# Partial sums of the Strassen products read out of one PSUM chain, the second row factor moved into the final norm, and no GpSimd sums in the feed-forward part

## The chip, the cores and the metric

The kernel runs on one core of a Trainium2 chip. The metric is the device time of one execution in microseconds. The engines are TensorE (PE; its weight loads are PEld), VectorE (DVE), ScalarE (ACT), GpSimd (POOL) and SyncE (SP), which issues the DMAs.

## What is computed

One decoder layer runs on 1024 prompt tokens and 8 sample tokens with common weights, T = 1032 columns in all: a mixer (pooling and convolution), cross attention, a gated feed-forward, and a final RMSNorm. The change lies in the last two:

```python
def rmsnorm(x, g):
    xf = x.astype(jnp.float32)
    y = xf * lax.rsqrt(jnp.mean(xf * xf, axis=-1, keepdims=True) + EPS)
    return (y * g.astype(jnp.float32)).astype(x.dtype)
...
    x = x + cross_attn(rmsnorm(x, g_attn), mk, mv, w_q, w_o)
    h = rmsnorm(x, g_ffn)
    x = x + (jax.nn.silu(h @ w_gate) * (h @ w_up)) @ w_down
...
y_prompt = rmsnorm(xp, g_final)
y_sample = rmsnorm(xs, g_final)
```

D_MODEL is 1024 and D_FF is 2816, that is FF_TILES = 22 tiles of 128.

## The kernel before, in words

**Layout.** Channels lie on the 128 partitions and tokens along the free axis. Every matrix operand is split into a high and a low half (`split`, L343 to L362: the high half by ScalarE at L351 or GpSimd at L353, the low half, a subtraction, at L362), and a product is three matmuls, one for each pair in `PASSES`. The tokens are cut in two column halves of 512 and 520.

**Feed-forward, first matrices.** Gate and up projections are done together as a 2 x 2 block product with seven products in place of eight. For each of the 22 tiles f, called a turn below, the seven are A11 and A12 (weights `wG`, 512 columns), S2 and S3 (`wTa`, 520), S1 and A22 (`wTb`, 520) and S4 (`wU`, 512). `ab` holds the seven token blocks, in the order A12, A22, S4, S1, A11, S2, S3 (0 to 6). `gate_prep` (L1261) and `sums_prep` (L1266) make the weights of one f from the loaded `gr`: four sums `ta`, `tb` by `minus` (L1278), then the splits.

A product of 512 columns is 12 matmuls into one bank of PSUM (`ms` tiles, of which there are two); one of 520 columns is 24 matmuls of 260 into two banks (`mm` tiles of three banks each, again two). Each of the seven has a tile of its own (`product`, L1315). ScalarE copies A11's sum into the tile `su` (L1340); VectorE adds each of the others to a part of `su` (`plus_sums`, L1336), S1's twice. When a quarter of `su` is complete, `gated` multiplies it by the row factor `Rf` (L1374; `Rf` is one over the root of the row's mean square, and comes from `rsqrt_rows` at L490 to L508), takes silu (ScalarE, L1381) and multiplies by `Rf` again. `times_value` multiplies the gate by the value, `combine` (L1348) forms the sums that the second matrix product needs, and `to_blocks` sends them to DRAM as `hb`, for an odd f as one transfer of four sums.

**Feed-forward, second matrix.** `w_down` goes through the same scheme. `down_sums` (L1458, L1464) forms its weight sums `ds` during the gate stage and sends them to DRAM as `td`. `down_block` loads the hidden sums `hs` back and splits them into tiles `hb`; `down_weights` loads and splits the weights `dr` into `dw`. The products run block by block (A11, S2, S3, S1, A22), four outputs p in each, then A12 and S4. `into` (L1336) adds them to the residual `x2`, which comes back from DRAM. The final norm is done in three column parts (`LAST_SPANS`: the second half first, then the first half in two). `square` (L1607 to L1616) takes the squares into `fin`, `rsqrt_rows` in its `direct` form makes the factor (ScalarE at L496, VectorE at L499 and L506 to L508), and `final` (L1623) multiplies and sends out. The first part's norm is put among the last products of A12 and S4; `last_units` (L1678, L1685) holds the other two.

**What sets the order.** `Program` is a planner in Python: tasks come in with the engines that may do them and a cost for each, and a list scheduler gives each to an engine, orders all of them by start time and priority (`BIAS` and `later` move priorities) and gives tiles from pools of fixed size (`op` 19, `scr` 3, `w` 2, `R` 1, `mm` 2, `ms` 2). Each engine's queue is then run in that order. Many sums may go to GpSimd or VectorE; the planner takes the one that is done first.

## Time and profile before

| what | value |
|---|---|
| runs of the kernel before | 1250.93 us median of 3 (1248.14 to 1252.08) |
| the profiled execution | 1248.25 us, of which the span from first to last instruction is 1246.5 us |
| mean granted TensorE clock | 0.992 |
| end of the last w_o matmul | 555.32 us after the span's start |
| gate stage, f = 1 to f = 21 | 599.90 to 1004.88 us (starts of S4's matmuls) |
| start of the down stage | 1007.66 us |

Times inside the execution count from the span's start. A group's row gives the line, engine, operation, tiles and shapes, then busy us and mean ns of one, then the idle time of the engine before such instructions and what ended it. A timeline's row gives start, duration and what ran; in brackets is the idle time before it and its releaser. A stretch's row has, for TensorE, weight loads, VectorE, ScalarE and GpSimd, the busy us and the number of instructions, then the granted clock, the share of the DMA engines and GB/s.

### The profile page before, as it was taken

To read this page: it belongs to the slowest core of one execution; us is meant where nothing else is said; L and a number is where in the kernel's file an instruction comes from. 1 tells how busy PE (TensorE), PEld (TensorE's weight loads), DVE (VectorE), ACT (ScalarE), POOL (GpSimd) and SP (SyncE) were. 2 spreads that over 40 slices of the span, in tenths; PEclk is the share of its full clock that TensorE was granted. 3 is DMA by queue.
4 is the path that set the end of the run, shared out by engine and by line. 5 is a ranking of instruction groups with operands and counts; after the bars stand their busy time and mean duration, and the time that the engine had idled before them with its cause. 6 is when DMAs were issued, how large, how long until landed. Compare 5 with 4: busy or idle time off the path is not lost.

```text
span 1246.5 us, 19894 instructions
## 1 busy us (share of the span) xinstructions
PE 1198.3 (96%) x7770; PEld 1125.7 (90%) x7770; DVE 953.8 (77%) x1490; ACT 497.9 (40%) x668; POOL 421.6 (34%) x397
## 2 busy tenths in 40 slices
...
GB/s 282 101 87 161 142 242 177 227 97 157 101 197 205 238 227 170 102 119 102 153 186 124 174 132 173 123 174 148 161 120 165 178 346 298 211 188 160 166 115 68
DMA packets 104334, 208.73 MB, mean 167 GB/s; under 512 B 10097, under 2 KB 53297, under 8 KB 102961
## 3 DMA queue, kind: packets, MB, share of 16 engines
...
q8 instruction: 61, 1.00, 0.3%
...
## 4 chain that ended last, share of the span: by engine, by line
PE 67%; DVE 17%; DMA 8%; issue 3%; ACT 3%; POOL 1%; SPq 1%; DVEq 0%; ACTq 0%; POOLq 0%
PE pr L1315 36%; PE ps L459 11%; PE po L459 7%; PE oa L459 4%; PE ob L459 4%; DVE su L1336 2%; DVE cacc L678 2%; DMA raw<-in_w_v 2%; DVE su L1374 1%; PE sc L1015 1%; PE fd L1678 1%; DMA spcache_k<-in_cache_k 1%; DMA gr<-in_w_gu 1%; DVE wG L362 1%; DVE spcache_k L1112 1%
## 5 line engine op out<-in xcount | busy, mean ns | idle before, releaser
L1315 PE MATMUL pr<-hb,dw 128*128 128x260 f32 (+1 forms) x1386 | 205.6, 310 | 3.2 <-DVE x L1336 2.5
L1315 PEld LDWEIGHTS pr<-hb,dw 128*128 128x128 f32 x1386 | 189.5, 189 | 19.1 <-ACT fin L496 3.5
L1315 PE MATMUL pr<-ab,wTb 128*128 128x260 f32 x1056 | 132.6, 283 | 6.0 <-DVE su L1336 6.0
L1315 PEld LDWEIGHTS pr<-ab,wTa 128*128 128x128 f32 x1056 | 132.0, 188 | 5.5 <-ACT wU L351 1.1
L1315 PEld LDWEIGHTS pr<-ab,wTb 128*128 128x128 f32 x1056 | 128.6, 188 | 8.0 <-DVE su L1336 7.9
L1315 PE MATMUL pr<-ab,wTa 128*128 128x260 f32 x1056 | 133.5, 282 | 1.5 <-DVE xa L1199 0.8
L1315 PE MATMUL pr<-ab,wG 128*128 128x512 f32 x528 | 128.8, 393 | 0.2 <-DVE Rf_m L499 0.2
L1336 DVE TENSOR_TENSOR su<-pr,su 128x520 f32<-128x520 f32 (+1 forms) x154 | 106.0, 689 | 28.1 <-PE pr L1315 26.9
L1315 PEld LDWEIGHTS pr<-ab,wG 128*128 128x128 f32 x528 | 97.8, 188 | 21.2 <-DVE Rf_m L499 0.3
L459 PE MATMUL ps<-xop,w 128*128 128x344 f32 x720 | 114.4, 320 | 0.9 <-DMA w<-in_w_in 0.9
L459 PEld LDWEIGHTS ps<-xop,w 128*128 128x128 f32 x720 | 113.5, 188 | 1.1 <-DMA w<-in_w_in 1.1
L459 PE MATMUL ps<-xq,w 128*128 128x344 f32 x576 | 94.9, 321 | 0.0
L459 PE MATMUL po<-oo,w 128*128 128x344 f32 x576 | 91.2, 320 | 0.4 <-DVE oo L1078 0.4
L459 PEld LDWEIGHTS po<-oo,w 128*128 128x128 f32 x576 | 90.9, 188 | 0.7 <-DVE oo L1078 0.7
L459 PEld LDWEIGHTS ps<-xq,w 128*128 128x128 f32 x576 | 90.8, 188 | 0.1
L678 DVE SCALAR_TENSOR_TENSOR cacc<-glu,vec,cacc 128x511 f32<-128x511 f32 (+14 forms) x116 | 77.0, 739 | 0.0
L351 ACT ACTIVATE wTa<-ta 128x1024 fp32r<-128x1024 f32 x21 | 22.3, 1063 | 123.1 <-DVE ta L1278 90.4
L1374 DVE TENSOR_TENSOR su<-su,Rf 128x512 f32<-128x512 f32 (+1 forms) x75 | 69.7, 930 | 1.3 <-ACT su L1381 0.5
L1315 PE MATMUL pr<-ab,wU 128*128 128x512 f32 x264 | 65.0, 395 | 0.0
L351 ACT ACTIVATE dw<-dr 128x1024 fp32r<-128x1024 f32 (+1 forms) x34 | 30.2, 898 | 84.0 <-PE pr L1315 65.4
L1336 DVE TENSOR_TENSOR x<-pr,x 128x520 f32<-128x520 f32 (+3 forms) x34 | 20.3, 628 | 55.0 <-PE pr L1315 47.7
L351 ACT ACTIVATE wG<-gr 128x1024 fp32r<-128x1024 f32 x21 | 22.3, 1062 | 96.9 <-PE pr L1315 87.6
...
## 6 DMA issues: line engine op xcount, KB each, us to landing
...
hb<-su SPq DMA_DIRECT2D x11, 1040.0 KB, 4.4
...
hs<-hb SPq DMA_DIRECT2D x20, 520.0 KB, 9.4
...
```

Source lines behind the costliest of these rows:

```text
L351: e.activation(dst(0), src(), AF.Copy, scale=1.0 if gain is None else gain)
L362: e.tensor_tensor(dst(1), src(), f32(dst(0)), ALU.subtract)
L459: e.matmul(ps[:, c, :CW], w[:, wi, cols], x[:, xi, c * CW : (c + 1) * CW], start=first and p == 0, stop=last and p == 2)
L678: e.scalar_tensor_tensor(acc[h][:, n:], src[:, : HALF - n], w, acc[h][:, n:], ALU.mult, ALU.add)
L1015: e.matmul(bank()[:, i * NMEM : (i + 1) * NMEM], qop[2 * h + dt][:, qi, tt * P : (tt + 1) * P], kk[:, ki, 2 * (h % 2) + dt], start=(dt == ...
L1112: e.scalar_tensor_tensor(piece[:, b], piece[:, b], 1.0, bc[:, b], ALU.mult, ALU.mult, accum_out=out(m)[:, first + b : first + b + 1])
L1315: e.matmul(t[:, c, :n] if banks == 2 else t[:, :n], weights(j, wi), xs[0](j, xi)[:, c * n : (c + 1) * n], start=j == 0 and p == 0, stop=j ...
L1336: from_sums(sums, width, "DVE", dve, lambda e, src, sl: e.tensor_tensor(as_banks(o(sl), src), src, as_banks(a(sl), src), ALU.add), [akey], ...
L1374: add({"Pool": pool_tt(n), "DVE": dve(n)}, lambda e: e.tensor_tensor(o(), o(), b(), ALU.mult), r + [(su[f], q)], [(su[f], q)], lock=True)
L1678: e.matmul(view(), weights(j, wi), moving(j, xi)[:, sl], start=j == 0 and n == 0, stop=j == PAIRS - 1 and n == 2)
```

## The change

It has five parts.

1. **Sums in PSUM.** A new class `Sums` lets several products add into the same tile. A11, S2, S3 and A22 of one f add up in one `mm` tile `chain`. After each of the first three ScalarE copies the sum so far into a quarter of `su`; after A22 VectorE multiplies the sum by `Rf` straight out of PSUM. S1 and S4 add up in the two `ms` tiles (`pieces`), read in halves of 260 and 252 or 260 columns: after S1 for the fourth quarter (`corner`), after S4 for the third (`third`). A12 takes the third bank of the chain's tile of the f before. A11 and S4 are now made of matmuls of 260 and 252 columns, 24 in place of 12; A11's block `ab` is widened to 520 columns with zeros.
2. **Order.** A turn is S2, S1, S3, corner, A11 of the next f, A22, S4, A12 of the next f.
3. **Row factor.** The second multiplication by `Rf` goes. Instead the residual `x2` is multiplied by the inverse of `Rf` when it comes back (eight VectorE products of 128x1032, at the start of the down stage). The final norm doesn't see a factor common to a row; its EPS is carried by starting `fin` from the squared inverse factor. The inverse, `rinv`, is made once, goes through DRAM, and takes `Rf`'s tile after the gate stage.
4. **No GpSimd sums.** From the end of the w_o loop on (`pg.alone`), a task that VectorE may do goes to VectorE alone. GpSimd keeps some splits, copies with a scale and memsets.
5. **Norm factors.** The three matmuls of `Rf` share one `mm` tile. For the final norm ScalarE reads PSUM first, without a bias, and VectorE's first step at L499 falls away; the first part of the final norm has one `mm` tile for both column pieces, behind S4's product. Down products of A12 go to `mm`, those of A11 alternate by p between `mm` and `ms`.

The diff, cut to its core:

```diff
@@ class Program
+        t.engines = {"DVE": engines["DVE"]} if self.alone and "DVE" in engines else engines
@@ rsqrt_rows, direct
+                add({"ACT": act(n, True)}, lambda e, ps=ps, dl=dl, n=n: e.activation(
+                    dst[:, dl], ps(n), AF.Abs_reciprocal_sqrt, scale=4.0), [psk], list(dkeys) + [yk], func=AF.Abs_reciprocal_sqrt)
+                add({"DVE": dve(n)}, lambda e, ps=ps, dl=dl, o=o, n=n: e.tensor_tensor(t(slice(o, o + n)), ps(n), dst[:, dl], ALU.mult),
+                    [psk, yk], [tk])
...
@@ products
+    class Sums:
+        def __init__(self, width, *tiles, first=0):
+            self.width, self.n = width, width if width <= 512 else width // 2
...
+    def product(weights, wkeys, xs, width, sums, steps=1):
...
+                    first = begin and j == 0 and p == 0
+                    for c in range(-(-width // n)):
+                        m = min(n, (sums.width if first else width) - c * n)
+                        e.matmul(sums.bank(c, m), weights(j, wi), xs[0](j, xi)[:, c * n : c * n + m],
+                                 start=first, stop=j == nj - 1 and p == 2, skip_group_check=True)
@@ gated
-        times(f, q, R, RF)
+        if sums is None:
+            times(f, q, R, RF)
+        else:
+            from_sums(sums, n, "DVE", dve, lambda e, src, sl: e.tensor_tensor(as_banks(o(sl), src), src, as_banks(R()[:, sl], src), ALU.mult), RF, [k])
         add({"ACT": act(n)}, lambda e: e.activation(o(), o(), AF.Silu), [k], [k], func=AF.Silu)
-        times(f, q, R, RF)
@@ the turn
+    def first(f):
+        su[f] = op_buf(f"su{f}", (P, 4, TW))
+        chain[f] = new_sums(TW, f"chain{f}")
+        copy_sums(lambda sl: su[f][:, 0, sl], (su[f], 0), of_tokens(gu_w[f][0], 0, A11, chain[f], 1 if f else 4))
+    def second(f):
+        sums = Sums(n, chain[f - 1].tiles[0], first=2) if f else new_sums(n, "second")
...
+    def fifth(f):
+        pieces[f] = of_tokens(gu_w[f][3], 0, S1, Sums(TW, *[ms_buf(f"pieces{f}_{c}") for c in range(2)]), 4 if not f else 1)
+    def seventh(f):
+        of_tokens(gu_w[f][2], 512, S3, chain[f], 4 if not f else 1)
+        copy_sums(part(f, 3), (su[f], 3), chain[f])
...
+        turns.append([(sixth, f), (fifth, f), (seventh, f), (corner, f), (first, f + 1), (fourth, f), (third, f), (second, f + 1)])
@@ down stage
+            add({"Pool": pool_tt(T), "DVE": dve(T)}, lambda e, i=i: e.tensor_tensor(x2[p][:, i], x2[p][:, i], rinv[:], ALU.mult),
...
+    pg.alone = True
...
+    add({"ACT": act(T)}, lambda e: e.activation(fin[:], rinv[:], AF.Square, scale=float(8 * EPS) ** 0.5), [(rinv,)],
@@ finish
+        wide = None if c else mm_buf("fin_ps", 2)
```

TensorE's queue in the middle of the gate stage, before (`pr` are the sums, one tile to a product; the number in `ab` is the block: 5 S2, 0 A12, 6 S3, 3 S1, 1 A22, 2 S4):

```order
L1315 MATMUL pr15_5695<-ab5_0_4738,wTa2_5614 128x260 x12
L1315 MATMUL pr15_5695<-ab5_1_5160,wTa2_5614 128x260 x12
L1315 MATMUL pr16_5732<-ab0_0_4678,wG2_5545 128x512 x6
L1315 MATMUL pr16_5732<-ab0_1_5065,wG2_5545 128x512 x6
L1315 MATMUL pr17_5754<-ab6_0_4741,wTa2_5614 128x260 x12
L1315 MATMUL pr17_5754<-ab6_1_5174,wTa2_5614 128x260 x12
L1315 MATMUL pr18_5786<-ab3_0_4727,wTb2_5619 128x260 x12
L1315 MATMUL pr18_5786<-ab3_1_5188,wTb2_5619 128x260 x12
L1315 MATMUL pr19_5819<-ab1_0_4689,wTb2_5619 128x260 x12
L1315 MATMUL pr19_5819<-ab1_1_5076,wTb2_5619 128x260 x12
L1315 MATMUL pr20_5856<-ab2_0_4756,wU2_5689 128x512 x6
L1315 MATMUL pr20_5856<-ab2_1_5200,wU2_5689 128x512 x6
```

The same queue now, with rows of S1 and of A11 (block 4) left out after the first:

```order
L1348 MATMUL chain19_9284<-ab0_0_4682,wG20_9422 128x512 x6
L1348 MATMUL chain19_9284<-ab0_1_5068,wG20_9422 128x512 x6
L1348 MATMUL chain20_9491<-ab5_0_4742,wTa20_9368 128x260 x12
L1348 MATMUL chain20_9491<-ab5_1_5163,wTa20_9368 128x260 x12
L1348 MATMUL pieces20_0_9629<-ab3_0_4731,wTb20_9458 128x260
...
L1348 MATMUL chain20_9491<-ab6_0_4745,wTa20_9368 128x260 x12
L1348 MATMUL chain20_9491<-ab6_1_5177,wTa20_9368 128x260 x12
L1348 MATMUL chain21_9683<-ab4_0_4382,wG21_9621 128x260 x3
...
L1348 MATMUL chain20_9491<-ab1_0_4693,wTb20_9458 128x260 x12
L1348 MATMUL chain20_9491<-ab1_1_5079,wTb20_9458 128x260 x12
L1348 MATMUL pieces20_0_9629<-ab2_0_4760,wU20_9587 128x260
```

S2, S3 and A22 go into one tile, and between two of them stands S1 or the next A11; S4 goes into S1's tiles.

ScalarE's queue there, before (L351 are splits, L1340 the copy of A11's sum, L1381 silu):

```order
L351 ACTIVATE wG19_8899<-gr19_0_8623 128x1024
L1381 ACTIVATE su18_8771<-su18_8771 128x512
L351 ACTIVATE wTb19_8933<-tb19_8774 128x1024
L351 ACTIVATE wTa20_8986<-ta20_8969 128x1024
L351 ACTIVATE wU19_9006<-gr19_1_8740 128x512
L1381 ACTIVATE su18_8771<-su18_8771 128x520
L1340 ACTIVATE su19_8936<-pr133_8993 128x512
```

And now (L349 splits, L1367 copies of the chain, L1408 silu):

```order
L349 ACTIVATE wG20_9422<-gr20_0_9194 128x1024
L1408 ACTIVATE su19_9342<-su19_9342 128x512
L1367 ACTIVATE su19_9342<-chain19_9284 128x520
L349 ACTIVATE wTb20_9458<-tb20_9310 128x1024
L1367 ACTIVATE su19_9342<-chain19_9284 128x520
L1367 ACTIVATE su20_9543<-chain20_9491 128x520
L349 ACTIVATE wTa21_9569<-ta21_9487 128x1024
```

Three copies stand where one stood: that of S2's sum behind silu, that of S3's behind the split of wTb.

TensorE's queue at the first part of the final norm, before (`pr174` is A12's product for p = 0, `pr175` S4's, `pr176` A12's for p = 1):

```order
L1315 MATMUL pr174_11206<-hb5_0_10944,dw20_8_11105 128x512 x3
L490 MATMUL fin0_ps0_11276<-fin_11020,ones_d_72 128x260
L493 MATMUL fin0_ps0_11276<-fsq0_7_11240,ones_d_72 128x260
L1315 MATMUL pr175_11297<-hb0_2_11027,dw21_0_11265 128x512 x6
...
L1315 MATMUL pr175_11297<-hb5_2_11250,dw21_8_11267 128x512 x3
L490 MATMUL fin0_ps260_11346<-fin_11020,ones_d_72 128x260
L493 MATMUL fin0_ps260_11346<-fsq0_7_11240,ones_d_72 128x260
L1315 MATMUL pr176_11361<-hb0_0_10842,dw22_0_11271 128x512 x6
```

And now:

```order
L1348 MATMUL d0_0_11597<-hb5_0_11334,dw20_8_11499 128x512 x3
L1348 MATMUL d2_0_11671<-hb0_2_11415,dw21_0_11657 128x512 x6
...
L1348 MATMUL d2_0_11671<-hb5_2_11641,dw21_8_11659 128x512 x3
L490 MATMUL fin_ps_11728<-fin_10089,ones_d_71 128x260
L493 MATMUL fin_ps_11728<-fsq0_7_11631,ones_d_71 128x260
L490 MATMUL fin_ps_11728<-fin_10089,ones_d_71 128x260
L493 MATMUL fin_ps_11728<-fsq0_7_11631,ones_d_71 128x260
L1348 MATMUL d0_1_11745<-hb0_0_11231,dw22_0_11663 128x512 x6
```

The norm's two pieces, which stood around S4's product with a tile each, stand together behind it in one tile.

More of the change, by code (lines that the diff above doesn't have):

```diff
@@ L50 @@
 LAST_SPANS = ((512, 520), (0, 256), (256, 256))
-BIAS = {"evac": 10, "prep": 20, "load": 0, "final": 40}
+BIAS = {"evac": 10, "prep": 20, "load": 0, "final": 40, "inverse": 60}
 ALL_SAMPLES = (1, 6, 7)
@@ L64 @@
 O_ORDER = (0, 4, 1, 5, 2, 6, 3, 7)
-AHEAD = 2
 PAIRS = FF_TILES // 2
@@ L487, in rsqrt_rows, with rows_of @@
         parts = [(o, min(step, width - o)) for o in range(0, width, step)]
-        for o, n in parts:
-            ps = ms_buf(f"{name}_ps{o}")
+        rows = {}
+        def rows_of(o, n):
+            rows[o] = ps, psk = psum(o) if psum else (lambda b: (lambda n: b[:, :n], (b,)))(ms_buf(f"{name}_ps{o}"))
             add({"PE": 0.1 + 0.0017 * n}, lambda e, ps=ps, o=o, n=n: e.matmul(
-                ps[:, :n], ones, total[:, lo + o : lo + o + n], start=True, stop=more is None), tkeys, [(ps,)])
+                ps(n), ones, total[:, lo + o : lo + o + n], start=True, stop=more is None), tkeys, [psk])
@@ L1206, in plain_block @@
     def plain_block(b, j, i, h):
-        split(lambda p: block(b, j, p), lambda p: bkey(b, j, p), lambda: quarter(j, i, h), HALF_WIDTH[h], [(xa[j], i, h)], gain=vcol(V_FFN, j + 4 * i))
+        split(lambda p: block(b, j, p)[:, : WIDTH[b]], lambda p: bkey(b, j, p), lambda: quarter(j, i, h), HALF_WIDTH[h], [(xa[j], i, h)],
+              gain=vcol(V_FFN, j + 4 * i))
+        if b == A11:
+            no_samples(lambda: f32(ab[b][j // 2][:, j % 2, :, HALF_WIDTH[0] :]), [bkey(b, j, p) + ("none",) for p in range(2)])
     def sum_blocks(j):
@@ L1577, in hybrid_step_kernel, with prepare @@
             gate_prep(1)
-    rsqrt_rows("Rf", Rf, RF, xss2, [(xss2,)], ones_d, 0, T)
-    for f in range(AHEAD):
-        first_two(f)
-    for f in range(FF_TILES):
-        if f + 1 < FF_TILES:
-            if f + 1 >= AHEAD:
-                later(lambda: gu_load(f + 1), "load")
-                later(lambda: gate_prep(f + 1))
-            later(lambda: sums_prep(f + 1))
+    pg.alone = True
+    ftmp = [scr(f"Rf_{i}", (P, 1, T)) for i in range(2)]
+    fps = mm_buf("Rf_ps")
+    rsqrt_rows("Rf", Rf, RF, xss2, [(xss2,)], ones_d, 0, T, tuple((t, 0) for t in ftmp), psum=lambda o: (lambda n: fps[:, o // 512, :n], (fps,)))
+    pg.later = BIAS["inverse"]
+    add({"DVE": dve(T)}, lambda e: e.scalar_tensor_tensor(ftmp[0][:, 0], ftmp[0][:, 0], -0.25, Rf[:], ALU.mult, ALU.mult),
+        RF + [(ftmp[0], 0, o) for o, _ in SPANS], [(ftmp[0], 0, o) for o, _ in SPANS], lock=True)
+    dma(lambda: rd, lambda: ftmp[0][:, 0], 4 * P * T, r=[(ftmp[0], 0, o) for o, _ in SPANS], w=[("rd",)])
+    pg.later = 0
+    first(0)
+    second(0)
+    def prepare(f):
+        if f < FF_TILES:
+            if f not in gu_raw:
+                later(lambda: gu_load(f), "load")
+                later(lambda: gate_prep(f))
+            later(lambda: sums_prep(f))
         else:
             fixed["DVE"] = 0.148
-        if f < AHEAD:
-            sixth(f)
-        else:
-            first_two(f, lambda: sixth(f))
-        others(f)
+    turns = []
+    for f in range(FF_TILES):
+        turns.append([(sixth, f), (fifth, f), (seventh, f), (corner, f), (first, f + 1), (fourth, f), (third, f), (second, f + 1)])
+    for f, turn in enumerate(turns):
+        prepare(f + 1)
+        for piece, g in turn:
+            if g < FF_TILES:
+                piece(g)
         down_sums(f)
     fin = buf("fin", "acc", (P, T))
+    dma(lambda: rinv[:], lambda: rd, 4 * P * T, r=[("rd",)], w=[(rinv,)])
+    add({"ACT": act(T)}, lambda e: e.activation(fin[:], rinv[:], AF.Square, scale=float(8 * EPS) ** 0.5), [(rinv,)],
+        [(fin, c) for c in range(len(LAST_SPANS))])
     last_sq = {}
@@ L1607, in square @@
             add({"ACT": act(width)}, lambda e: e.activation(sq[:], x2[j][:, i, sl], AF.Square), xk, [(sq,)])
-        elif n == 0:
-            add({"ACT": act(width)}, lambda e: e.activation(fin[:, sl], x2[j][:, i, sl], AF.Square), xk, fk)
         else:
@@ L1639, in run @@
                 x2_load(p)
-            sums = product(weights, wkeys, hidden(b), WIDTH[b], len(GROUPS) if (b, p) == (A11, 0) else 1)
+            sums = product(weights, wkeys, hidden(b), WIDTH[b], new_sums(WIDTH[b], f"d{b}_{p}", p), len(GROUPS) if (b, p) == (A11, 0) else 1)
             if b in (A11, S2):
```

140 lines of the change are left out of this document (68 added, 72 removed).

## Prediction

> **What bounds the kernel now.** I read the busy shares first, then the timeline of TensorE, then the table of stretches. The first (busy us, share of the span):
>
> ```profile
> PE 1198.3 (96%) x7770; PEld 1125.7 (90%) x7770; DVE 953.8 (77%) x1490; ACT 497.9 (40%) x668; POOL 421.6 (34%) x397
> ```
>
> TensorE is the bound, and the change removes no matmul. So it can only win TensorE's idle time or its slow clock. Up to the last w_o matmul all engines keep their instructions in their order; what follows counts. Timeline of TensorE there (start, duration, in brackets the idle time before it and who ended it):
>
> ```profile
> 543.80 11.52 PE L459 MATMUL po<-oo,w 128*128 128x344 f32 x72
> ...
> 556.16 2.40 PE L1315 MATMUL pr<-ab,wTa 128*128 128x260 f32 x18 [0.84 <-DVE xa L1199]
> 561.06 1.98 PE L490 MATMUL Rf_ps<-xss,ones_d 128*128 128x512 f32 x4 [2.50 <-DVE xss L389]
> 563.60 0.39 PE L490 MATMUL Rf_ps<-xss,ones_d 128*128 128x8 f32 x2 [0.55 <-DVE Rf_m L499]
> ...
> 588.33 5.98 PE L1315 MATMUL pr<-ab,wTa 128*128 128x260 f32 x48 [0.64 <-DVE su L1336]
> ...
> 599.90 2.96 PE L1315 MATMUL pr<-ab,wU 128*128 128x512 f32 x12
> ```
>
> Call 555.32 (the end of the first row) to 599.90 the boundary. The gate stage follows, a turn for each f:
>
> ```profile
> 637.23 3.14 PE L1315 MATMUL pr<-ab,wTb 128*128 128x260 f32 x24 [0.41 <-DVE su L1336]
> 640.21 2.94 PE L1315 MATMUL pr<-ab,wU 128*128 128x512 f32 x12
> ...
> 648.64 2.96 PE L1315 MATMUL pr<-ab,wG 128*128 128x512 f32 x12
> 651.43 3.03 PE L1315 MATMUL pr<-ab,wTa 128*128 128x260 f32 x24
> 654.30 5.91 PE L1315 MATMUL pr<-ab,wTb 128*128 128x260 f32 x48
> 660.05 2.26 PE L1315 MATMUL pr<-ab,wU 128*128 128x512 f32 x9
> ...
> 1004.88 2.94 PE L1315 MATMUL pr<-ab,wU 128*128 128x512 f32 x12
> ```
>
> From start to start a product of 12 wide matmuls takes 2.79 us (648.64 to 651.43), one of 24 narrow ones 2.87 (654.30 to 660.05, halved). The turn from 640.21 to 660.05 had no wait: 19.84 us. From 599.90 to 1004.88 there are 20 turns in 404.98 us, where 20 x 19.84 = 396.8. So waits cost 8.2 us there, nearly all of one kind: TensorE waits until VectorE has read a sum out of PSUM (the row at 637.23).
>
> **The change part by part.**
>
> *Turns.* A11, S2, S3 and A22 now add up in one tile, and each next product waits until the sum before it was read. The order puts other work between: S1 (2.87) while ScalarE copies S2's sum, A11 of the next f (2.79) while it copies S3's, S4 (2.79) while VectorE reads A22's. The prices and the load of VectorE:
>
> ```profile
> L1336 DVE TENSOR_TENSOR su<-pr,su 128x520 f32<-128x520 f32 x98 | 67.7, 691 | 5.8 <-PE pr L1315 5.0
> ...
> L1374 DVE TENSOR_TENSOR su<-su,Rf 128x512 f32<-128x512 f32 x39 | 40.9, 1049 | 0.7
> ...
> L1336 DVE TENSOR_TENSOR su<-pr,su 128x512 f32<-128x512 f32 x40 | 27.4, 685 | 20.2 <-PE pr L1315 20.1
> L362 POOL TENSOR_TENSOR wTb<-tb,wTb 128x1024 fp32r<-128x1024 f32 x9 | 25.0, 2779 | 0.8
> ...
> L1374 DVE TENSOR_TENSOR su<-su,Rf 128x520 f32<-128x520 f32 x30 | 21.9, 728 | 0.5 <-ACT su L1381 0.5
> ...
> L351 ACT ACTIVATE wTa<-ta 128x1024 fp32r<-128x1024 f32 x19 | 20.2, 1063 | 115.3 <-DVE ta L1278 90.4 <-PE pr L1315 24.9
> ...
> L362 DVE TENSOR_TENSOR wTb<-tb,wTb 128x1024 fp32r<-128x1024 f32 x11 | 14.0, 1274 | 7.1 <-ACT wTb L351 5.7 <-POOL wTb L353 1.4
> ...
> L1340 ACT ACTIVATE su<-pr 128x512 f32<-128x512 f32 x20 | 12.0, 598 | 23.4 <-PE pr L1315 23.4
> ```
>
> ```profile
> 600.00:700.00 100.00, 98.43 (x652) 90.19 (x651) 88.43 (x125) 24.50 (x32) 36.85 (x32) 1.00 0.50 169
> 700.00:800.00 100.00, 98.08 (x647) 89.67 (x645) 87.09 (x112) 25.19 (x32) 40.52 (x34) 1.00 0.45 148
> 800.00:900.00 100.00, 99.36 (x659) 91.31 (x660) 85.37 (x118) 26.00 (x33) 35.60 (x31) 1.00 0.45 151
> 900.00:1000.00 100.00, 98.64 (x654) 90.46 (x653) 84.66 (x111) 25.87 (x34) 38.26 (x31) 1.00 0.50 161
> ```
>
> (The table has TensorE, weight loads, VectorE, ScalarE, GpSimd.) A copy is 0.60 us, and the two more per turn raise ScalarE from 5 to some 6.3 of 20 us. It may stand behind a weight split (1.06) in ScalarE's queue: 1.7 us, still under 2.79. VectorE loses much: the four groups of sums and Rf products are 157.9 us for 20 turns; after, a turn has one sum of A12, one Rf product in SBUF, one out of PSUM (0.69 each) and four half-wide pieces (0.42, as the half-wide read in the tail's rows below): 3.8 us, 76 in all, so 82 us go. In exchange GpSimd's sums come over. GpSimd is busy 151 us there, and VectorE does the same task in half the time (wTb 2779 against 1274 ns): at most 76 us. So VectorE stays below the 345.6 us it has now, some 16 of 20 us per turn, and collisions with GpSimd end too (1049 ns against 728 for the same product). Waits can remain where VectorE's queue is late, from nothing to 4 us; I take 2, a quarter of today's. **-8.2 + 2.0 = -6.2.**
>
> A rule speaks against this part. The Trainium skill, Perfetto Trace Analysis, Matmuls under Optimizing Tensor Performance, has independent matmul groups rotate through PSUM banks, so that reading one overlaps the next; a chain in one bank is the opposite. Its reading of this case is rival 1.
>
> *Form.* A11 and S4 go from 12 matmuls of 512 to 24 of 260 and 252. The nearest rows are 2.79 (same columns, half the count) and 2.87 (same count, 8 columns more), so each of 44 products costs 0 to 0.08 more; the middle makes **+1.8** (0 to 3.5).
>
> *Boundary.* Its 44.58 us hold 5 wide products (13.9), 8 narrow ones (23.0) and the Rf matmuls (2.4): 39.3, so 5.3 us are lost. After, TensorE starts with 9 of A12(0)'s 12 matmuls and all of A11(0): 4.9 us, to 560.2, and the Rf matmuls still can't start before 561.06, as xss comes then: 0.8 lost. The three of them now share a tile, and the two waits on Rf_m go. New: S3(0) and A22(0) follow their predecessor with little between, so that two copies show, at 0.60 and an estimated 0.15 of handover each, and perhaps the reads of S1's pieces (0.4). I put 2.7 lost: **-2.6** (0 to -4).
>
> *Start of the down stage.* Now:
>
> ```profile
> 1007.66 23.14 PE L1315 MATMUL pr<-hb,dw 128*128 128x512 f32 x99
> 1031.24 4.93 PE L1315 MATMUL pr<-hb,dw 128*128 128x512 f32 x20 [0.44 <-DVE x L1336]
> ...
> 1190.90 1.24 DVE L1623 TENSOR_TENSOR x<-x,fin 128x1040 f32<-128x1040 f32 x1
> ```
>
> VectorE gets eight products of x2 with the inverse factor, 128x1032; the nearest row is 1.24 us, 9.9 in all, and the sums GpSimd did. Between 1010 and 1050 its queue gets nearly full. The A11 products now alternate between both kinds of PSUM tile, so four sums can wait instead of two. I take **+0.6** (-0.5 to +4).
>
> *First part of the final norm.* Now, TensorE, then two stretches (granted clock after the five engines), then ScalarE:
>
> ```profile
> 1173.33 0.60 PE L490 MATMUL fin_ps<-fin,ones_d 128*128 128x260 f32 x2
> 1173.76 0.60 PE L493 MATMUL fin_ps<-fsq,ones_d 128*128 128x260 f32 x2
> 1176.42 9.44 PE L1315 MATMUL pr<-hb,dw 128*128 128x512 f32 x33 [2.05 <-DVE x L1336]
> 1186.64 0.71 PE L490 MATMUL fin_ps<-fin,ones_d 128*128 128x260 f32 x2 [0.78 <-DVE x L1336]
> ...
> 1188.53 3.72 PE L1315 MATMUL pr<-hb,dw 128*128 128x512 f32 x15 [0.74 <-DVE fin_m L499]
> ```
>
> ```profile
> 1177.00:1179.00 2.00, 2.00 (x8) 1.52 (x7) 0.00 (x0) 0.70 (x1) 1.98 (x1) 0.64 0.63 185
> 1179.00:1181.00 2.00, 2.00 (x6) 1.61 (x5) 0.46 (x1) 1.06 (x1) 0.40 (x1) 0.51 0.01 2
> ```
>
> The sums of this norm and the products of A12 and S4 share two PSUM tiles, so TensorE idles 2.05, 0.78 and 0.74 us. After the first wait the clock is at 0.64 and 0.51, and 33 matmuls take 9.44 us instead of 33/12 x 2.79 = 7.67. Lost: 3.6 + 1.8 = 5.4. After, both parts share one larger tile of their own and stand behind S4's product, whose weights are split by then: **-5.4** (-2 if weights come late and TensorE idles anyway).
>
> The Trainium skill, TensorE: Matmul & The Clock Gate, Part 1, lets the clock fall only after an idle window of about 3.4 us. The row shows it fallen after 2.05 us of wait with 1.2 us of small matmuls before; by the page the slow stretch has another cause and may stay, and this term would be -3.6.
>
> *Tail.* Of the last norm's chain VectorE's first step goes, for which ScalarE waits:
>
> ```profile
> 1237.56 0.42 DVE L499 TENSOR_SCALAR fin_m<-fin_ps 128x256 f32<-128x256 f32 x1 [1.24 <-PE fin_ps L493]
> ...
> 1238.02 0.48 ACT L496 ACTIVATE fin<-fin_ps,eps 128x256 f32<-128x256 f32 x1 [0.71 <-DVE fin_m L499]
> ```
>
> ScalarE starts 0.46 earlier, and all behind it: **-0.5**.
>
> Sum: -6.2 + 1.8 - 2.6 + 0.6 - 5.4 - 0.5 = -12.3. The profiled execution took 1248.25 us (span 1246.5), 2.7 below the median of the runs, 1250.93, and within their spread; 1248.25 - 12.3 = 1236.0 is its counterpart, and against the median it makes **1238.6**.
>
> **The rivals.**
> 1. *The chain's reads show.* If in each turn one of the copies comes late by the length of a copy, 22 x 0.6 = 13 us eat the gain: about 1251, no change. For it: the queues of ScalarE and VectorE are in order, and copies stand behind splits. Against: 2.8 us of cover each. Were both copies bare, as the rule on banks has it for a chain, 2 x 0.75 x 22 = 33 us would be lost, 1272; only the first turn is built like that.
> 2. *A transfer holds two queues: slower.* In every second turn the split of wTb needs the tile that a transfer of four sums frees. Its low half stands on VectorE ahead of the reads of S1's pieces, for which S4 waits.
>
> ```profile
> hb<-su SPq DMA_DIRECT2D x11, 1040.0 KB, 4.4
> ...
> hs<-hb SPq DMA_DIRECT2D x20, 520.0 KB, 9.4
> ```
>
>    Counted from the end of a turn's S4: A12's sum is there after 2.8 us and the last of the four sums some 1.5 later, at 4.3; with 4.4 the transfer has landed at 8.7; the two halves of the split end at 11.0, and two sums and the two reads (2.2) at 13.2. S4 is due after A12, S2, S1, S3, A11 and A22, at 2 x 2.79 + 4 x 2.87 = 17.1. So 3.9 us of cover are left, and the mechanism decides from a landing of 8.3 us on. At the 9.4 of the other row, 11 x 1.1 = 12 us are lost, 1251; at 10.5, 24 us and 1263. Against: 9.4 belongs to a stretch in which DMA is full; in this stage it is half busy (0.45 to 0.50 in the stretches).
> 3. *VectorE is full at the start of the down stage*: its 9.9 us and GpSimd's sums push A11's and S2's products back by 4 to 8 us instead of 0.6: 1242 to 1246.
> 4. *Part of the loss at the first final norm stays*: the idle time, if it is the weights', 1242; the slow clock alone, if it has another cause than the idle time, 1240.4.
>
> **How the numbers follow.** The forecast, waits of 0 to 4 us in the gate stage included, has 0.62; rivals 1 to 4 have 0.13, 0.08, 0.10 and 0.07. The low end takes every term at its good end (-8.2, 0, -4, -0.5, -5.4, -0.5: 1232.3, the run's own scatter inside); the high end reaches over rivals 3 and 4 into rival 1, to 1249. 0.3% is 3.8 us, about what a measurement of this kernel can tell from no change: faster than 1247.2 are the forecast, rivals 3 and 4 and a little of 1, 0.79; within it 0.12; slower 0.09.
>
> **What would show it.** TensorE's waits from 600 to 1005 us below 3 us in sum, a turn of 19.9 to 20.0 us; no wait over 0.5 us and a clock of 1.00 around the first final norm; two short waits on ScalarE's copies in the first turn. It is wrong if waits on ScalarE's copies recur in each turn, if ScalarE waits there on the transfer of hidden sums for over 2 us, or if VectorE has no idle time after 1010 us and TensorE waits for x.

## The result, and the profile after

The changed kernel takes 1236.24 us (median of 4 runs, 1234.77 to 1241.29), the kernel before 1251.51 us beside it (1248.14 to 1252.28): ratio 0.989, 95% interval 0.9856 to 0.9925. The prediction was 1238.6 us (1232.3 to 1249.0).

The profiled execution of the changed kernel is the longest of its four, 1241.29 us with a span of 1239.4. In it the last w_o matmul ends at 561.30 us, in the one of before at 555.32, though nothing is changed up to there. So both are compared from that point on: 691.18 us to the end before, 678.10 now, 13.1 less, where the prediction had 12.3. (The medians lie 15.3 us apart: the profiled execution of before was one of its faster ones, as e5 shows.) By parts:

| stretch | before | after | forecast | measured |
|---|---|---|---|---|
| end of w_o to the end of S4 of f = 1 | 47.37 | 44.09 | -2.4 | -3.3 |
| from there to the first matmul of the down stage (20 turns) | 404.97 | 402.55 | -4.6 | -2.4 |
| to the first matmul of the final norm, S4's product taken out | 165.67 | 165.04 | +0.6 | -0.6 |
| first part of the norm, with S4's product for p = 0 | 15.20 | 9.23 | -5.4 | -6.0 |
| from there to the end | 57.97 | 57.19 | -0.5 | -0.8 |

(In the second column the product A11 of f = 2, 2.84 us, which now stands ahead of the first mark, and six matmuls of the down stage that fill a gap, 1.38 us, are counted where they stood before. Of the form's +1.8 the first stretch has 0.2, the second 1.6.)

The busy shares after, from the page:

```profile
PE 1201.9 (97%) x8298; PEld 1154.8 (93%) x8298; DVE 898.1 (72%) x1546; ACT 533.6 (43%) x725; POOL 200.7 (16%) x229
```

VectorE has lost 56 us and GpSimd 221. TensorE's timeline at the boundary and in a turn (start, duration, idle before and its releaser):

```profile
561.15 2.22 PE L1348 MATMUL second<-ab,wG 128*128 128x512 f32 x9
...
567.15 2.08 PE L490 MATMUL Rf_ps<-xss,ones_d 128*128 128x512 f32 x6 [0.49 <-DVE xss L387]
...
582.52 3.13 PE L1348 MATMUL chain<-ab,wTb 128*128 128x260 f32 x24 [0.69 <-ACT su L1367]
...
608.23 2.94 PE L1348 MATMUL chain<-ab,wG 128*128 128x512 f32 x12
611.01 3.04 PE L1348 MATMUL chain<-ab,wTa 128*128 128x260 f32 x24
613.88 3.04 PE L1348 MATMUL pieces<-ab,wTb 128*128 128x260 f32 x24
616.76 3.05 PE L1348 MATMUL chain<-ab,wTa 128*128 128x260 f32 x24
619.65 3.00 PE L1348 MATMUL chain<-ab,wG 128*128 128x260 f32 x24
622.49 3.02 PE L1348 MATMUL chain<-ab,wTb 128*128 128x260 f32 x24
625.34 3.00 PE L1348 MATMUL pieces<-ab,wU 128*128 128x260 f32 x24
628.17 2.94 PE L1348 MATMUL chain<-ab,wG 128*128 128x512 f32 x12
...
709.74 3.04 PE L1348 MATMUL chain<-ab,wG 128*128 128x512 f32 x12 [0.65 <-DVE su L1407]
```

At the boundary the wait for xss is 0.49 us instead of 2.50, and of the two copies that follow closely one shows, 0.69. The turn from 608.23 to 628.17 has no wait: 19.94 us, 0.10 more than before's 19.84, which is the new form of two products (2.84 instead of 2.79 each). The reader should see that S2, S3 and A22 write one tile and yet follow each other without idle time. Twenty such turns are 398.8 us, so 3.75 of the 402.55 are lost to waits; before it was 8.2. (The idle time itself sums to 2.3 us in 5 waits; a product that has waited also takes some 0.3 us longer.) What is left is one kind, the row at 709.74: A12 waits until VectorE has read the chain. VectorE just before it:

```profile
707.73 0.89 DVE L1495 TENSOR_TENSOR ds<-ds 128x256 f32<-128x256 f32 x2 [1.56 <-DMA ds<-in_w_dn]
708.65 0.42 DVE L1501 SCALAR_TENSOR_TENSOR ds<-ds 128x256 f32<-128x256 f32 x1
708.99 0.69 DVE L1407 TENSOR_TENSOR su<-chain,Rf 128x520 f32<-128x520 f32 x1
```

Three sums of w_down stand ahead of the read in VectorE's queue, and they wait 1.56 us for their own transfer. All five waits lie between 648 and 811.4 us, and the last sum of w_down begins at 810.3. The start of the down stage and the first norm:

```profile
1009.32 40.95 PE L1348 MATMUL d<-hb,dw 128*128 128x512 f32 x222
...
1180.65 0.60 PE L490 MATMUL fin_ps<-fin,ones_d 128*128 128x260 f32 x2
...
1181.96 0.60 PE L493 MATMUL fin_ps<-fsq,ones_d 128*128 128x260 f32 x2
1182.21 30.74 PE L1348 MATMUL d<-hb,dw 128*128 128x512 f32 x132
```

TensorE has no wait left in either.

### The profile page after: what moved, and what is told of

Same layout as the page of the kernel before. It is cut to its first block, busy times and chain, and to the rows that moved or that the text cites. A ratio compares the mean times of both kernels' runs of the same rounds, so it can differ in the third digit from the quotient of the medians.

```text
span 1239.4 us, 20723 instructions
## 1 busy us (share of the span) xinstructions
PE 1201.9 (97%) x8298; PEld 1154.8 (93%) x8298; DVE 898.1 (72%) x1546; ACT 533.6 (43%) x725; POOL 200.7 (16%) x229
## 4 chain that ended last, share of the span: by engine, by line
PE 68%; DVE 14%; DMA 11%; issue 3%; ACT 2%; SPq 1%; POOL 0%; DVEq 0%; ACTq 0%; POOLq 0%
PE d L1348 16%; PE chain L1348 13%; PE ps L457 12%; PE po L457 7%; PE pieces L1348 5%; DMA td<-ds 4%; PE oa L457 4%; PE ob L457 4%; DMA ds<-in_w_dn 4%; DVE cacc L687 2%; DVE ds L1495 2%; PE pv L1082 2%; PE sc L1024 2%; DMA raw<-in_w_v 2%; PE fd L1734 1%
## 5 line engine op out<-in xcount | busy, mean ns | idle before, releaser
L1348 PE MATMUL d<-hb,dw 128*128 128x260 f32 (+1 forms) x1386 | 203.8, 309 | 0.0
L1348 PEld LDWEIGHTS d<-hb,dw 128*128 128x128 f32 x1386 | 188.7, 188 | 14.1
L1348 PE MATMUL chain<-ab,wTa 128*128 128x260 f32 x1056 | 133.9, 283 | 0.0
L1348 PEld LDWEIGHTS chain<-ab,wTa 128*128 128x128 f32 x1056 | 131.0, 189 | 2.1 <-ACT su L1367 0.2
L1348 PE MATMUL chain<-ab,wG 128*128 128x260 f32 (+2 forms) x780 | 128.7, 319 | 2.4 <-DVE su L1407 2.3
L1348 PEld LDWEIGHTS chain<-ab,wG 128*128 128x128 f32 x780 | 109.9, 189 | 13.1 <-DVE su L1407 3.4
L351 POOL TENSOR_SCALAR dw<-dr 128x384 fp32r<-128x384 f32 (+1 forms) x16 | 9.6, 597 | 517.4 <-DVE su L1407 393.2
L1367 ACT ACTIVATE su<-chain 128x520 f32<-128x520 f32 x66 | 39.5, 600 | 69.8 <-PE chain L1348 69.8
L349 ACT ACTIVATE dw<-dr 128x1024 fp32r<-128x1024 f32 (+1 forms) x40 | 34.8, 881 | 77.6 <-PE d L1348 63.6
L1348 PE MATMUL chain<-ab,wTb 128*128 128x260 f32 x528 | 66.6, 282 | 0.7 <-ACT su L1367 0.7
L1348 PE MATMUL pieces<-ab,wTb 128*128 128x260 f32 x528 | 66.9, 282 | 0.0
L1348 PE MATMUL pieces<-ab,wU 128*128 128x260 f32 (+1 forms) x528 | 65.9, 281 | 0.0
L1348 PEld LDWEIGHTS pieces<-ab,wTb 128*128 128x128 f32 x528 | 64.9, 189 | 0.1
```

The lines of the kernel that those rows point to most:

```text
L349: e.activation(dst(0), src(), AF.Copy, scale=1.0 if gain is None else gain)
L351: e.tensor_scalar(dst(0), src(), 1.0 if gain is None else gain, 1.0, ALU.mult, ALU.mult)
L1348: e.matmul(sums.bank(c, m), weights(j, wi), xs[0](j, xi)[:, c * n : c * n + m], start=first, stop=j == nj - 1 and p == 2, skip_group_check ...
L1367: from_sums(sums, sums.width, "ACT", lambda n: act(n, True), lambda e, src, sl: e.activation(as_banks(o(sl), src), src, AF.Copy), [], [okey])
```

## The experiments

Times are read from each profile in two stretches, since the part up to the end of w_o is the same in all and varies by itself. In the changed kernel and what is made from it the first stretch holds 1.4 us of down products that fill a gap (2.8 in e4).

| kernel | end of w_o to down stage | down stage to end | ratio to before (interval) |
|---|---|---|---|
| before, first and second profile | 452.3, 458.5 | 238.8, 237.1 | 0.9998 (0.9978 to 1.0018) |
| changed | 448.0 | 230.1 | 0.989 (0.9856 to 0.9925) |
| e1 changed, GpSimd back | 451.3 | 230.3 | 0.9919 (0.9897 to 0.9941) |
| e2 changed, old norm tiles | 446.7 | 230.2 | 0.9877 (0.9852 to 0.9901) |
| e3 before, norm tile | 458.4 | 232.2 | 0.9981 (0.9956 to 1.0006) |
| e4 changed, bare chain | 500.2 | 228.4 | 1.0297 (1.0257 to 1.0338) |
| e6 before, no GpSimd sums | 444.1 | 236.5 | 0.9883 (0.986 to 0.9906) |
| e7 changed, both row factors | 444.0 | 229.9 | 0.9825 (0.9802 to 0.9848) |
| e8 changed, w_down sums behind the read | 444.0 | 230.1 | 0.9829 (0.9803 to 0.9854) |
| e9 before, e6 and e3 together | 443.1 | 233.2 | 0.9858 (0.9831 to 0.9885) |
| e10 e6 with idle GpSimd work | 469.0 | 237.3 | 1.010 (1.0068 to 1.0132) |
| e11 changed, hidden sums sent three times | 448.9 | 229.9 | 0.9876 (0.9834 to 0.9918) |

### e1: GpSimd may take sums again

```diff
-    pg.alone = True
```

> The changed kernel, but GpSimd may take sums again. Theory A (what helps in the gate stage is that VectorE has fewer and undisturbed sums): VectorE's sums next to GpSimd's get longer again, TensorE's lost time between 600 and 1005 us goes from 3.7 to 6-9 us, the run takes 3 to 5 us more than the changed kernel, ratio to before about 0.992. Theory B (what is left of the waits is the queue of the sums of w_down ahead of the gated read on VectorE): GpSimd takes part of those sums, VectorE reads the chain in time, TensorE's lost time falls to 1-2 us, 2 us less than the changed kernel, ratio 0.987.

1240.09 us, ratio 0.9919. TensorE's waits on the gated read and on ScalarE's copies in the gate stage and at the boundary sum to 3.4 and 1.9 us, and the first stretch is 3.3 us longer. Counted like the 3.75 us above, the turns lose 7.1 us. Theory A's size held. Theory B fell in this form: GpSimd took some of the sums (it is busy for 91 us between 600 and 1000 us instead of 3), and the waits didn't go. The number to keep for later: with the chain, the new order and the lighter VectorE, but with GpSimd's sums, the turns still lose 7.1 us, against 8.2 and 13.2 in the two profiles of the kernel before.

### e2: the first norm with its old tiles

```diff
-        wide = None if c else mm_buf("fin_ps", 2)
+        wide = None
...
-        psum = None if c else lambda o: (lambda n: wide[:, int(o > 0), :n], (wide,))
+        psum = None
```

> The changed kernel, but the first part of the final norm has two tiles of one bank, shared with S4's product, as before. If the loss there came from the tiles (theory): TensorE waits 1 to 3 us around the two small pieces, the clock falls behind a wait of 2 us, the run takes 3 to 6 us more than the changed kernel, ratio about 0.993. If it came from late weights (rival): no difference, waits stay under 0.5 us, ratio 0.989.

1235.47 us, ratio 0.9877: no difference. TensorE there:

```profile
1175.03 0.60 PE L490 MATMUL fin_ps<-fin,ones_d 128*128 128x260 f32 x2
1175.47 0.60 PE L493 MATMUL fin_ps<-fsq,ones_d 128*128 128x260 f32 x2
1175.71 7.95 PE L1348 MATMUL d<-hb,dw 128*128 128x512 f32 x33
1183.50 0.60 PE L490 MATMUL fin_ps<-fin,ones_d 128*128 128x260 f32 x2
1183.93 0.60 PE L493 MATMUL fin_ps<-fsq,ones_d 128*128 128x260 f32 x2
```

The two pieces stand around S4's product again, each with an `ms` tile, and nothing waits. So the common tile isn't needed in the changed kernel. That doesn't make late weights the cause, as the rival would have it: the changed kernel also puts A12's products into `mm` tiles, so that only S4's product shares the `ms` tiles with the norm. e3 tells the two apart.

### e3: the kernel before, with the norm's common tile alone

```diff
+        wide = mm_buf(f"{name}_ps", 2) if direct and width > 512 else None
...
-            ps = ms_buf(f"{name}_ps{o}")
+            ps = ms_buf(f"{name}_ps{o}") if wide is None else wide
```

> The kernel before with one thing changed: both pieces of the first final norm share one tile of two banks of their own, so that the products of A12 and S4 keep the two others. Theory: the waits of 2.05 and 0.78 us go, with them the clock of 0.64 and 0.51; at least 4 of the 5.4 us are won, ratio 0.996. Rival 1 (weights): TensorE waits as long, for a split of weights: ratio 1.000. Rival 2 (the slow clock has another cause than the idle time): waits gone, clock still slow, 3.6 us won, ratio 0.997.

```profile
1179.58 0.60 PE L498 MATMUL fin_ps<-fin,ones_d 128*128 128x260 f32 x2
1180.02 0.60 PE L501 MATMUL fin_ps<-fsq,ones_d 128*128 128x260 f32 x2
1180.27 7.99 PE L1331 MATMUL pr<-hb,dw 128*128 128x512 f32 x33
1188.10 0.60 PE L498 MATMUL fin_ps<-fin,ones_d 128*128 128x260 f32 x2
```

The waits are gone with the weights where they were, and the second stretch is 232.2 us against 238.8 and 237.1. So the loss came from three users of two tiles; either more tiles for the norm or other tiles for A12 cures it. The ratio, 0.9981 (0.9956 to 1.0006), shows 2 us less, which the interval doesn't tell from none: the first stretch of this profile, whose order is that of before, was 6 us longer than in the first profile of before and as long as in the second (e5).

### e4: the chain without cover

```diff
-        turns.append([(sixth, f), (fifth, f), (seventh, f), (corner, f), (first, f + 1), (fourth, f), (third, f), (second, f + 1)])
+        turns.append([(fifth, f), (sixth, f), (seventh, f), (corner, f), (fourth, f), (first, f + 1), (third, f), (second, f + 1)])
```

Two added dependencies (A11 behind the A22 before it, S2 behind S1) hold the planner to that order.

> The changed kernel with the order of a turn changed by two added dependencies: S1, then S2, S3 and A22 with nothing between, then A11 of the next f, S4, A12. Theory (the cover between them makes the chain free): each of two copies a turn is bare, 0.60 us and 0.15 of handover, TensorE loses 2 x 0.75 x 22 = 33 us more, about 1269 us. Rival (ScalarE's copy overlaps with the next product's first matmuls or the reads cost little): under 15 us more, below 1252 us.

1287.4 us. The waits table and the timeline of TensorE:

```profile
PE chain L1348 <- ACT su L1367: 36.3, 42, 3.0
```

```profile
711.69 3.03 PE L1348 MATMUL chain<-ab,wTa 128*128 128x260 f32 x24
715.50 3.14 PE L1348 MATMUL chain<-ab,wTa 128*128 128x260 f32 x24 [0.78 <-ACT su L1367]
719.34 3.13 PE L1348 MATMUL chain<-ab,wTb 128*128 128x260 f32 x24 [0.69 <-ACT su L1367]
```

Both copies of a turn are bare: 42 waits, 36.3 us. From start to start a product that waits takes 3.81 to 3.84 us instead of 2.87, so a copy costs 0.95, not 0.75. Of the 51 us over the changed kernel, 7.6 are lost by the first S4 (31.8 us after w_o's end, 24.2 in the changed kernel); 40 of the waits lie behind it, at 0.95 us 38, and the rest is a few longer waits and a stretch of half clock. The theory's 1269 us was too low by the same terms. Rival 1 of the prediction priced a real danger, and the order of the turn is what removes it. The Trainium skill, Perfetto Trace Analysis, Matmuls under Optimizing Tensor Performance, has independent matmul groups rotate through PSUM banks, so that reading one overlaps the next. The trace agrees: products in other banks cover the copies in the changed kernel, and each copy shows here, where nothing stands between.

### e5: the kernel before once more

> The kernel before, unchanged, profiled once more, since its runs spread over 11 us and the first profile is one of them. Theory (the spread lies in the gate stage's waits and in the stall at the first final norm, both races between queues): the stretch from the end of w_o to the start of the down stage comes out several us away from 452.3 us, and the stretch from there to the end several us below 238.8 if the clock doesn't fall. Rival (the spread lies in the unchanged part or in the clock): both stretches within 1 us of the first profile. Ratio 1.000.

1253.21 us, ratio 0.9998. Its waits in the gate stage sum to 9.9 us in 10 instances (6.7 in the first profile, the longest 3.3 against 1.2), the first stretch is 458.5, 6.2 us more than in the first profile. Some 3 of them are idle time. The rest is mostly the clock, which is at half twice, in the wait for xss (2.54 us) and behind the longest wait of the turns; in the first profile it is at 1.00 in both places:

```profile
560.80:564.20 3.40, 2.96 (x4) 1.29 (x5) 3.01 (x5) 0.73 (x1) 0.00 (x0) 0.51 0.46 187
642.70:646.20 3.50, 3.50 (x18) 3.40 (x17) 2.13 (x4) 0.26 (x1) 1.27 (x1) 0.51 0.25 70
```

```profile
641.42 4.49 PE L1315 MATMUL pr<-ab,wTb 128*128 128x260 f32 x24 [3.33 <-DVE su L1336]
```

So the kernel before varies by several us in the very waits that the change removes, and in the slow clock that may follow them. At the first norm:

```profile
1182.63 7.86 PE L1315 MATMUL pr<-hb,dw 128*128 128x512 f32 x33 [2.15 <-DVE x L1336]
1191.28 0.71 PE L490 MATMUL fin_ps<-fin,ones_d 128*128 128x260 f32 x2 [0.78 <-DVE x L1336]
```

The wait is as long as in the first profile, 2.15 us, but the 33 matmuls take 7.86 and not 9.44 us, and the clock stays at 1.00. The first profile in steps of 1 us (the column behind GpSimd's is the granted clock):

```profile
1176.00:1177.00 1.00, 0.58 (x3) 0.52 (x4) 0.27 (x1) 0.81 (x3) 0.94 (x1) 1.00 0.83 192
1177.00:1178.00 1.00, 1.00 (x5) 0.81 (x4) 0.00 (x0) 0.70 (x1) 0.98 (x1) 0.78 1.00 296
...
1180.00:1181.00 1.00, 1.00 (x4) 0.81 (x3) 0.46 (x1) 0.50 (x1) 0.00 (x0) 0.51 0.00 0
1181.00:1182.00 1.00, 1.00 (x6) 0.79 (x6) 0.76 (x1) 0.00 (x0) 0.00 (x0) 1.00 0.00 0
```

Half speed for about 3.4 us after a wait of 2.05 us, and none after one of 2.15: among waits of this length, the length doesn't decide. Over all profiles of this document, TensorE has nine waits of 1.9 to 2.6 us behind w_o; six go with half clock for 3.4 us or a multiple of it, three do not. The four longer ones (2.97 to 11.9 us) all do, no shorter one does, and the six runs whose waits there stay under 1.5 us have a clock of 1.00 from w_o's end to TensorE's last product. So it was chance that the first profile lost 1.8 us at this place; what the change removes are the waits, and with them the risk of such a loss at each of them.

### e6: the kernel before, without sums on GpSimd

```diff
+        t.engines = {"DVE": engines["DVE"]} if self.alone and "DVE" in engines else engines
...
+    pg.alone = True
     rsqrt_rows("Rf", Rf, RF, xss2, [(xss2,)], ones_d, 0, T)
```

> The kernel before with the fourth part of the change alone: from the end of w_o on no sums on GpSimd. Theory (GpSimd can only be freed because VectorE lost its second products and its sums): VectorE goes from 17.3 to over 18 us of a 20 us turn, TensorE's waits in the gate stage rise, the run is 2 to 8 us longer, ratio 1.002 to 1.006. Rival (the collisions of the two engines are the cost): VectorE's load falls, the waits halve, 4 us shorter, ratio 0.997.

1238.48 us, ratio 0.9883: as much as the whole change. My theory fell, and the rival was right in sign and too small. VectorE does more, as expected, and TensorE doesn't wait in the turns at all; the table of stretches (TensorE, weight loads, VectorE, ScalarE, GpSimd):

```profile
600.00:700.00 100.00, 100.00 (x669) 92.19 (x669) 92.24 (x152) 26.92 (x34) 3.15 (x8) 1.00 0.53 172
700.00:800.00 100.00, 100.00 (x670) 92.22 (x669) 87.70 (x142) 24.82 (x32) 3.74 (x8) 1.00 0.47 151
```

TensorE is busy without a gap from 600 to 1000 us, with VectorE at 86 to 92 of 100 us. It had waited, with VectorE at 85 to 88, while GpSimd worked. From 600 to 1000 us GpSimd falls from 151 to 15 us, and VectorE, which takes over its sums, rises only from 346 to 354: its own work got shorter, the product with the row factor for one from 1049 to 743 ns:

```profile
L1374 DVE TENSOR_TENSOR su<-su,Rf 128x512 f32<-128x512 f32 x40 | 29.7, 743 | 0.6
```

### e7: the second row factor put back

```diff
         add({"ACT": act(n)}, lambda e: e.activation(o(), o(), AF.Silu), [k], [k], func=AF.Silu)
+        times(f, q, R, RF)
...
-            add({"Pool": pool_tt(T), "DVE": dve(T)}, lambda e, i=i: e.tensor_tensor(x2[p][:, i], x2[p][:, i], rinv[:], ALU.mult),
...
-    rinv = buf("rinv", "R", (P, T))
```

`fin` then starts from a constant that carries EPS.

> The changed kernel with the second multiplication by the row factor put back and the eight products of x2 with the inverse left out. Theory (VectorE has room since the sums moved into PSUM, and the factor is not what pays): VectorE about 1.4 us more per turn, TensorE's waits in the gate stage 0 to 3 us more, time 0 to 3 us over the changed kernel, ratio 0.989 to 0.992. Rival (dropping the factor is what relieves the gate stage): waits at 8 us again, 5 us or more over, ratio 0.994.

1232.09 us, ratio 0.9825, and its interval lies below that of the changed kernel, which neither side had expected. VectorE has 76 to 81 of 100 us in the first three hundreds of the gate stage, and TensorE doesn't wait there. The dropped factor is not what pays. Why this kernel doesn't have the changed kernel's waits is only argued: other tasks on VectorE let the planner place the sums of w_down elsewhere (the last begins at 870 us instead of 810, and VectorE waits 4.4 us for their transfers instead of 15.4).

### e8: the sums of w_down behind the gated read

```diff
-        minus(3, 3, 1)
-        minus(1, 1, 0)
+        minus(3, 3, 1, first=[("gate", n * DS_TURNS // 10)])
+        minus(1, 1, 0, first=[("gate", n * DS_TURNS // 10)])
```

> The changed kernel with one added dependency: the sums of w_down number n wait for the gated read of turn 0.8 n, so that on VectorE they stand behind it instead of ahead of it, where they wait for their own transfer. Theory (this queue makes all waits left in the gate stage): no wait on the gated read any more, from the end of w_o to the start of the down stage 3 us less than 448.0, ratio 0.987. Rival (the wait moves on: to the reads of S1's pieces, or the weights of S2 in the down stage come late): no gain, or 1 to 4 us more.

1231.55 us, ratio 0.9829, and the first stretch is 444.0 us, 4.0 less. No wait on the gated read is left: the changed kernel's remaining waits were this queue. The gain is larger than the theory's 3 us and 0.987. The sums are spread over more turns (the last begins at 916 us instead of 810), and none reaches the down stage. There VectorE is as full as in the changed kernel; the row of that comes first, that of e8 second:

```profile
1010.00:1050.00 40.00, 40.00 (x220) 34.49 (x219) 37.96 (x44) 21.29 (x27) 3.77 (x2) 1.00 0.92 367
1010.00:1050.00 40.00, 40.00 (x260) 36.34 (x260) 37.52 (x42) 16.86 (x23) 2.57 (x2) 1.00 0.87 336
```

TensorE has no gap in either: with VectorE at 38 of 40 us, the sums of the down products could wait, which the prediction's third rival denied.

### e9: e6 and e3 together

Both diffs on the kernel before.

> The kernel before with two parts of the change: no sums on GpSimd from the end of w_o on, and one tile of two banks for the first final norm; own PSUM tiles, the old order of a turn and both row factors stay. Theory (these two are the gain; chain, order and dropped factor pay at the boundary what the new form costs): 444 us from the end of w_o to the start of the down stage, 231 from there to the end, ratio 0.982 to 0.985, 4 to 7 us under the changed kernel. Rival (the two gains overlap, since VectorE is fuller in the down stage): ratio 0.988 as with the first part alone.

1236.03 us, ratio 0.9858; the first stretch is 443.1, the second 233.2 us, 2 more than expected. By the intervals it can't be told from the changed kernel, nor from e6 or e8. With two small edits the kernel before gets what the whole change gets, as far as these intervals can tell.

### e10: idle work for GpSimd

Eight additions on a tile of its own follow a memset that GpSimd does in each turn; the queues of the four others keep their order.

```diff
+            for _ in range(8):
+                e.tensor_tensor(spare[:], spare[:], spare[:], ALU.add)
```

> The kernel before without sums on GpSimd, to which idle work is given: eight additions of 128x256 on a tile of its own in each turn, which nothing waits for; all other queues keep their order. Theory 1 (what made TensorE wait is collisions: VectorE's sums of two SBUF tiles take longer while GpSimd reads SBUF): VectorE's means rise by 10 to 30%, TensorE loses 4 us or more in the gate stage, ratio 0.992 to 0.997. Theory 2 (GpSimd's slow sums were links in chains on which VectorE waited): no wait returns, within 1 us of the kernel without the idle work, ratio 0.988.

1265.5 us, ratio 1.010, much more than either theory had. From the first S4 to the down stage it takes 426.8 us (42.2 to 469.0), e6 413.7 (30.4 to 444.1): 13 us more. VectorE's groups between 600 and 1000 us in e6, then in e10:

```profile
L1336 DVE TENSOR_TENSOR su<-pr,su 128x520 f32<-128x520 f32 x102 | 70.6, 692 | 7.6 <-PE pr L1315 7.6
...
L1458 DVE TENSOR_TENSOR ds<-ds 128x256 f32<-128x256 f32 x63 | 26.4, 419 | 3.4 <-DMA ds<-in_w_dn 2.7
...
L1278 DVE TENSOR_TENSOR tb<-gr,ta 128x512 f32<-128x512 f32 x20 | 13.7, 684 | 0.0
```

```profile
L1336 DVE TENSOR_TENSOR su<-pr,su 128x520 f32<-128x520 f32 x99 | 68.0, 687 | 0.0
L1467 DVE TENSOR_TENSOR ds<-ds 128x256 f32<-128x256 f32 x61 | 34.5, 566 | 11.2 <-DMA ds<-in_w_dn 8.4 <-issue 2.2
...
L1278 DVE TENSOR_TENSOR ta<-tb,gr 128x512 f32<-128x512 f32 x20 | 20.7, 1034 | 0.0
L1278 DVE TENSOR_TENSOR tb<-gr,ta 128x512 f32<-128x512 f32 x20 | 16.9, 845 | 0.0
```

```profile
600.00:700.00 100.00, 98.22 (x653) 89.85 (x652) 96.15 (x145) 24.16 (x31) 48.15 (x47) 1.00 0.49 159
```

The groups `ds`, `ta` and `tb<-gr,ta`, which have two SBUF inputs, take 24 to 51% longer (419 to 566 ns, 684 to 1034 and 845), the sum that reads PSUM and SBUF stays at 690, VectorE is at 94 to 96 of 100 us, and waits of TensorE on VectorE's sums are back (7.8 us in 10 instances). Nothing waits for the idle work itself, and VectorE waits for GpSimd's splits no longer than in e6 (0.3 us from 605 to 1000 us). So theory 1 holds in its mechanism: collisions alone bring the waits back. The Trainium skill, SBUF — State Buffer, Who interferes with whom, says that a VectorE instruction with two SBUF inputs contends with a GpSimd instruction that reads SBUF, and that one with at most one, outside the two-port modes, does not. The trace agrees. Not every group that meets the idle work is stretched: `tb<-gr,gr` stays at 675 ns, and at 655.1 us it is GpSimd's addition beside it that takes 1.13 us instead of 0.61.

The other 12 us are lost at the boundary and are another thing: a split that GpSimd does there stands behind two blocks of the idle work in GpSimd's queue, and VectorE waits 10.0 us for it. TensorE then waits 11.9 us for xss instead of 2.5, with half clock behind it (0.51 from 572 to 582 us). The 1.010 as a whole is therefore no price of collisions.

### e11: three transfers for one

```diff
+        for _ in range(3 if count == 4 else 1):
+            one_to_blocks(c, j, first, count, width, src, keys)
```

> The changed kernel, but each transfer of four hidden sums is made three times, so that the tile comes free later. By the prediction's second rival a landing beyond 8.3 us costs its excess 11 times: if the third transfer lands at about 10 to 11 us, TensorE loses 19 to 30 us, in waits on S1's pieces, ratio above 1.00. If the cover is larger than counted there: ratio under 0.995.

1238.28 us, ratio 0.9876: no loss. The page's row for the 33 transfers, and ScalarE's waits:

```profile
hb<-su SPq DMA_DIRECT2D x33, 1040.0 KB, 5.7
```

```profile
ACT wTb L349 <- DMA hb<-su: 12.6, 9, 2.7
```

The landing is a median of single transfers, 5.7 us, and ScalarE waited less for them than in the changed kernel, where it was 52 us in 19 instances, probably because the planner, which knows of the longer transfers, gave the splits other tiles. So this run doesn't measure the cover of the prediction's second rival; it shows only that three times the traffic did no harm. The changed kernel itself says more: its transfers land after 5.6 us, ScalarE waits 52 us for them and VectorE 60.7 us behind ScalarE's split, and TensorE doesn't wait once for a read of S1's pieces.

## Why the prediction was right, and where it was not

**The sum.** 13.1 us against 12.3, which is in part luck: the turns gave 2.2 us less than forecast, the four other parts together 3.0 more.

**Turns.** Right in sign, 2.2 us too high in size (-4.6 against -2.4): the waits left are 3.75 us, not 2, and the form took 0.4 more. The chain's cover held as worked out: no wait on a copy in the steady turns, and e4 shows what it would cost without. The step that failed is the reason given. The prediction put the gain down to VectorE's lighter load, 82 us of sums and products that go, and to reads with other work between; that collisions with GpSimd end was a clause at the end. The load did fall, further than forecast, to 14 of 20 us (283 of 400) where the prediction had some 16. But with this lighter load and GpSimd's sums the turns still lose 7.1 us (e1). And e6 turns the reason round: without any of the new tiles, orders or dropped products, with VectorE fuller than before, the waits go when GpSimd's sums go, and e10 brings them back with work that only collides. What the prediction listed as a cost (GpSimd's sums come over to VectorE, "at most 76 us") was the gain. In the kernel before GpSimd's slow sums were also links on which VectorE waited (7.1 us for `tb` between 600 and 1000 us); how the 8 us divide between the two is open.

**What is left in the turns** was foreseen as "where VectorE's queue is late"; e8 shows the place: the sums of w_down, which wait for their transfer ahead of the gated read.

**Form.** Forecast 0.04 for each product, measured 0.05 (2.84 against 2.79 us).

**Boundary.** -3.3 against -2.4. One copy showed instead of two (0.69), and the Rf matmuls, which now follow each other in one tile, took 1.9 us instead of 2.4. xss came when forecast, 5.7 us after w_o's end in both kernels. The 0.15 us of handover that the prediction put beside a copy comes from no run; e4 shows 0.35.

**Start of the down stage.** -0.6 against +0.6. VectorE was nearly full, as forecast (38 of 40 us), but the sums could wait: no gap of TensorE from 1009 to 1182 us.

**First norm.** -6.0 against -5.4, from the right cause (e3), though the common tile was one of two cures (e2). The part of the clock, 1.8 of the 5.4, was in the profiled execution and not at this place in the other (e5), so counting it in full was luck; the rest, 3.6, is what the change removes for certain. In e6 the wait of 2.05 us goes without any new tile, and the two others stay, 0.78 and 0.68 us.

**Tail.** -0.8 against -0.5, not taken apart.

**Rivals.** The first (copies show) didn't come about, and the third's full VectorE did, but cost TensorE nothing. For the second, e11 was no test; the prediction's own sign of it, ScalarE waiting for the hidden sums for over 2 us, came plainly (52 us) and was no sign of harm: the landing of 5.6 us lies under the 8.3 where harm was to begin, and no read of S1's pieces came late. In the fourth the idle time was not the weights' (e3). The slow clock went with waits of TensorE, but among those of about 2 us not with each (e5).

Put together: the change's two paying parts are no sums on GpSimd and enough tiles for the first norm (e9: 0.9858). Chain, order and dropped factor bring 3.3 us at the boundary, cost 2.0 in form and, through VectorE's queue, waits of 3.75, which e7 and e8 remove. e7 and e8, at 0.9825 and 0.9829, beat both kernels. What the chain alone would give the kernel before, without its other parts, was not run.
